# A split-precision encoder layer: the first phase reordered, and the parts of split products taken in another order

## The chip, the cores and the metric

The kernel runs on one core of a Trainium2 chip. The number that counts is the time of one execution on the device, in microseconds (us). A core has several engines that run side by side, each through its own list of instructions in order: TensorE for matrix products (PE in the profile, and PEld for its loads of stationary operands), VectorE (DVE), ScalarE (ACT), GpSimd (POOL) and SyncE (SP), which mostly sends for transfers. Sixteen DMA engines carry the transfers. TensorE writes its results to PSUM, eight banks of 128 partitions by 512 float32 numbers; all other data stand in the larger SBUF or in DRAM.

## The reference

Two sequences (here batch 0 and batch 1) of 1024 rows and 1024 channels go separately through one layer:

```python
xn = rmsnorm(x, g_pre)
p = xn @ w_in                                  # 8192 columns
fv, fg, hv, hg, mg = split(p)                  # 1024, 1024, 3072, 1024, 2048
fz = fft over the sequence and over groups of 256 channels, of fv; real part
y_f = (fz * silu(fg)) @ w_fourier_out
hv = short_conv(hv, w_short); v, x1, x2 = split(hv)
z = v
for n, gate in enumerate((x1, x2)):
    z = gate * long_conv(z, kf[:, n], hyena_d[n])   # over 2L points
y_h = (z * silu(hg)) @ w_hyena_out
g_f, g_h = split(sigmoid(mg + b_merge))
out = (g_f * y_f + g_h * y_h) @ w_out
return x + rmsnorm(out, g_post)
```

The filters kf come from a small network over positions (two hidden layers with a sine each, then exponentials), transformed to frequencies.

## The kernel before

**Split products.** Every large product is made of float32 operands cut in two: a rounded part h, made by ACT (`copy`, a CAST in the profile), and the remainder l = source - h, made by DVE or POOL (a TENSOR_TENSOR at line 181). `split` (L168) does both and keeps the ACT instruction as `self.rounded`. A product is then three passes of TensorE: weight h on data h, weight h on data l, weight l on data h. `mm3` (L372) issues the three, for one block of 128 inner channels after the other, and so before the change the remainder of the weight is needed two products after its rounded part.

**The phases, in order.** `phase_fourier` (L486) makes the Fourier branch of both batches and the hidden layers of the filter network. `phase_main` (L868) makes the filters, with some of the gate projections between them, and then calls `branches` (L908): 32 convolutions (two batches, two orders, eight channel tiles). One convolution is `conv_front` (transposes and butterflies on DVE) and `conv_back` (L796), which calls `forward` (L593, frequency products pX, with DVE's bh and bl as data), multiplies by the filter, splits the result into yh and yl, and goes back with products pT. Its input comes from `inproj` (L727): a PSUM tile pin of 1024 columns, weights wh and wl, data xh and xl, which `load_x` (L714) makes of the normalized, transposed x (d_x in DRAM); the tiles of x are loaded anew for the second batch. `phase_gates` (L996) makes gate projections of batch 1 by a seven-product scheme (`times`, L979, PSUM tile pg). `phase_out` (L1108) makes the two output projections of the branches (`project`, L1147, pyf and pyh) and, in `last_rows`, the last projection and norm.

**The Fourier phase.** It works in five steps for each batch b.

- `norm` (L303) loads the eight row blocks of x (128 rows each), squares each on ACT (Square with a sum, output sq), makes the reciprocal roots of four sums at a time on DVE (`rstd`), and writes eight diagonal matrices dg. For batch 0 the row blocks stay in SBUF; for batch 1 they pass through three buffers of the tag "x".
- `xtile` (L327), once for each of eight channel tiles k, multiplies eight 128-column blocks of x by the diagonals on TensorE (tpx: transposes and scales at once), evicts them on ACT as xg (two buffers, which the outputs sq of `norm` share), writes xg to d_x over SP's queue, folds the sequence into even and odd halves eo on DVE, and splits these into eh and el. Row 512 of the sequence is kept apart in x5, by two very small DVE operations for each k.
- `weights` (L360) loads 128 rows of the Fourier weights (wfv), folds them into wer and wor, and splits these into the resident even and odd weights we and wo. There are two halves of the weights; batch 0 takes half 0 and then half 1, batch 1 takes half 1, which is still there, and then half 0 again.
- `pfv` (L378) adds the 3 products of one channel tile to one of eight sums for each half: e = 0 (even, four row tiles m) and e = 1 (odd, four). For batch 0 and half 0 six sums are begun within the loop over channel tiles: the four even ones in the four "mm" banks and two odd ones in the two "X" banks, while the transposes tpx use the two "T" banks. For batch 1 nothing is begun; there tpx uses the "mm" banks. The sums not begun follow in `fourier_half` (L383).
- `fourier_half` splits the sums as they close, adds a product pfx of x5 with the even weights, evicts that as x5t, and goes through the sequence stages (`stage`, L420: PSUM tiles pse and pso, eviction sev, result sst, products with the large table seq) and the channel stages (pP, pQ, with the table chan; DVE makes fA and fB, which POOL's queue writes to d_fz).

`hidden` (L273) makes one hidden layer of the filter network: two products phd, seven DVE operations each and a Sin on ACT, at the end of which SP's queue writes it to DRAM. Layer 0 stands at the very start, layer 1 after the last half of batch 1. The tables seq, alt, chan and chx are sent for on POOL's queue and vec on SP's, all in the code after the loop of batch 0; a one-column POOL copy into seq and into chan, which reads the last row scales, holds these two back until the norm is done.

**What sets the order of the work.** Not the code's order alone: a planner simulates the program and lists each engine's instructions by when they could start in the simulation, with program order between equals. `tc.issue_after(ins)` keeps instructions from being listed before another one. In the kernel before, the whole second `norm` stands in `issue_after(behind.ins)`, where `behind` is the last rounding of the weights of half 1 (L514, L540). Transfers that one engine sends for go through its queue in the order of its list: SP's queue carries x, wfv, d_x and later nearly all loads; POOL's carries tables, d_fz and weights of the later phases; ACT's queue carries two small loads at the start.

## Time and profile before

| | |
|---|---|
| median of 3 runs | 2446.82 us (2443.44 to 2447.43) |
| the profiled execution | 2449.26 us, of it 2447.1 us span |
| PE busy | 2396.1 us, 98% of the span |
| PEld busy | 2082.3 us, 85% |
| DVE busy | 1893.8 us, 77% |
| ACT busy | 1096.8 us, 45% |
| POOL busy | 485.9 us, 20% |
| Transfers | 429.36 MB, mean 175 GB/s |

The span runs from the first to the last instruction that the profile records; the time of the execution is a little longer. The Fourier phase takes the first 224 us of the span. Busy shares are means over the whole span, and stages differ, so stretches of it have to be read one by one.

A row for a group of instructions reads: source line, engine, operation, output<-input, partitions x elements and type, count, then busy us in all and the mean ns of one, and then the idle time of that engine just before them with what ended it. A row for one instruction begins with its start in us and its duration in us, and ends with the idle time before it and what released it. A row for a stretch has its bounds, its length, the busy us of PE, PEld, DVE, ACT and POOL (with counts), the granted TensorE clock, the busy share of the DMA engines and the GB/s moved. A row of waits has the engine, the waiting tile and line, what released it, and then the total, count and longest in us. A row of the chain has a start, a duration and the work that the end depended on. A row for transfers has the count, the size of one, and the median us from its issue to its landing.

### The profile page before, as it was taken

Reading aid. Unit: us, or ns where it says so; the run is one execution under the profiler, and the core shown is the slowest. Engines: PE = TensorE matmul, PEld = TensorE weight load, DVE = VectorE, ACT = ScalarE, POOL = GpSimd, SP = SyncE. Lnnn points to the kernel's source line nnn. Section 1 sums busy time; section 2 is a strip of 40 time slices with the busy share of each in tenths; the row PEclk is TensorE's granted clock in tenths of the full one; section 3 lists DMA queues with packets and bytes.
Section 4 is the critical chain, followed back from the end, with each engine's and each line's share of the span. In section 5 each row is a group of like instructions: output and inputs, shape, how many; then the busy total and the mean of one; then the engine's idle time right before and its main releaser. Section 6 shows DMA issues by size and latency. Waiting matters only on the chain.

```text
span 2447.1 us, 36853 instructions
## 1 busy us (share of the span) xinstructions
PE 2396.1 (98%) x13196; PEld 2082.3 (85%) x13196; DVE 1893.8 (77%) x3405; ACT 1096.8 (45%) x2063; POOL 485.9 (20%) x516
## 2 busy tenths in 40 slices
PE   6999999999999999999999999999999999999998
PEld 5988888888888888888888888888788888888886
DVE  7687888888748999999989999766555455665677
ACT  5545677767633433334223333333344444544343
POOL 1341222222143433331000000112200111122111
PEclk9999999999999999999999999999999999999999
DMA  7545655555555555445434444335454567776543
GB/s 273 170 141 191 224 175 173 167 175 167 173 194 177 172 177 173 165 165 192 146 128 134 141 141 138 121 121 184 154 174 159 198 210 255 245 250 213 169 164 129
DMA packets 225151, 429.36 MB, mean 175 GB/s; under 512 B 23542, under 2 KB 87255, under 8 KB 224456
## 3 DMA queue, kind: packets, MB, share of 16 engines
q1 hardware_dynamic: 198444, 333.34, 41.1%
q0 software_dynamic: 26336, 93.65, 10.9%
q8 instruction: 104, 1.70, 0.3%
q14 instruction: 79, 0.65, 0.1%
q10 hardware_dynamic: 188, 0.02, 0.0%
HBM read 290.60 MB, written 136.31 MB: 174 GB/s over the span
## 4 chain that ended last, share of the span: by engine, by line
PE 88%; DMA 5%; issue 3%; DVE 2%; ACT 1%; POOL 1%; SPq 0%; DVEq 0%; POOLq 0%; ACTq 0%
PE pin L194 41%; PE pT L194 7%; PE pg L194 7%; PE pX L194 7%; PE po L194 6%; PE pyh L194 5%; PE pyf L194 5%; PE pXf L194 3%; PE pfv L194 2%; DMA wr<-in_w_fo 1%; PE pft L194 1%; PE tph L792 1%; DMA wr<-in_w_ho 1%; PE tpx L194 1%; DMA wfv<-in_w_fv 1%
## 5 line engine op out<-in xcount | busy, mean ns | idle before, releaser
L194 PE MATMUL pin<-xh,wl 128*128 128x512 f32 x1472 | 577.2, 392 | 2.6 <-POOL wl L181 2.6
L194 PE MATMUL pin<-xl,wh 128*128 128x512 f32 x1472 | 575.6, 391 | 2.4 <-DVE xl L181 2.4
L194 PE MATMUL pin<-xh,wh 128*128 128x512 f32 x1472 | 576.5, 392 | 0.7 <-DMA wh<-d_w 0.7
L181 POOL TENSOR_TENSOR wl<-wr,wh 128x512 fp32r<-128x512 f32 x136 | 240.3, 1768 | 1144.0 <-ACT wh L171 1105.9
L194 PEld LDWEIGHTS pin<-xh,wl 128*128 128x128 f32 x1472 | 277.1, 188 | 54.9 <-POOL wl L181 4.1
L194 PEld LDWEIGHTS pin<-xl,wh 128*128 128x128 f32 x1472 | 277.1, 188 | 54.3 <-DVE xl L181 3.2
L194 PEld LDWEIGHTS pin<-xh,wh 128*128 128x128 f32 x1472 | 277.1, 188 | 52.1 <-DMA wh<-d_w 1.1
L171 ACT CAST wh<-wr 128x512 fp32r<-128x512 f32 x264 | 162.8, 619 | 346.0 <-PE pin L194 136.8
L194 PE MATMUL pT<-cinv,yh 128*128 128x256 f32 x1024 | 193.1, 283 | 0.0
L194 PEld LDWEIGHTS pT<-cinv,yh 128*128 128x128 f32 x1024 | 164.0, 190 | 9.0
L181 DVE TENSOR_TENSOR t<-pX,k 128x1024 f32<-128x1024 f32 x128 | 155.9, 1218 | 10.9 <-PE pX L194 9.3
L194 PE MATMUL pX<-bh,cfwd 128*128 128x256 f32 x768 | 159.6, 286 | 0.0
L181 DVE TENSOR_TENSOR wl<-wr,wh 128x512 fp32r<-128x512 f32 x128 | 87.2, 687 | 93.5 <-ACT wh L171 93.2
L194 PE MATMUL pyf<-sf,wh 128*128 128x512 f32 x512 | 158.0, 390 | 0.9 <-ACT wh L171 0.9
L194 PE MATMUL pyh<-sh,wh 128*128 128x512 f32 x512 | 157.3, 389 | 0.0
L171 ACT CAST bh<-b 128x512 fp32r<-128x512 f32 x144 | 89.0, 620 | 126.7 <-DVE b L181 84.5
L194 PE MATMUL pT<-cinv,yl 128*128 128x256 f32 x512 | 144.9, 283 | 0.0
L171 ACT CAST yh<-y 128x512 fp32r<-128x512 f32 x128 | 79.2, 619 | 114.1 <-DVE y L181 91.3
L194 PEld LDWEIGHTS pX<-bh,cfwd 128*128 128x128 f32 x768 | 126.3, 190 | 2.5
L194 PEld LDWEIGHTS pyf<-sf,wh 128*128 128x128 f32 x512 | 96.0, 188 | 21.3 <-ACT wh L171 1.6
L194 PEld LDWEIGHTS pyh<-sh,wh 128*128 128x128 f32 x512 | 96.1, 188 | 19.9
L194 PE MATMUL pX<-bl,cfwd 128*128 128x256 f32 x384 | 109.6, 285 | 0.0
(354 smaller groups left out, 5262.7 us busy)
## 6 DMA issues: line engine op xcount, KB each, us to landing
k<-d_k SPq DMA_DIRECT2D x128, 512.0 KB, 4.0
wr<-in_w_in SPq DMA_DIRECT2D x136, 256.0 KB, 3.1
d_g<-gt SPq DMA_DIRECT2D x124, 256.0 KB, 2.6
d_k<-kt SPq DMA_DIRECT2D x128, 128.0 KB, 2.1
d_k<-kt SPq DMA_DIRECT2D x64, 256.0 KB, 2.3
wr<-in_w_fo POOLq DMA_DIRECT2D x64, 256.0 KB, 4.0
g<-d_g SPq DMA_DIRECT2D x64, 256.0 KB, 4.2
wr<-in_w_ho POOLq DMA_DIRECT2D x64, 256.0 KB, 3.7
```

Of the source, the lines that this page charges most:

```text
L171: self.rounded = nc.scalar.copy(h, src)
L181: return e.tensor_tensor(out, a, b, op=op)
L194: return self.nc.tensor.matmul(out, lhsT, rhs, start=start, stop=stop, skip_group_check=shared)
L792: nc.tensor.transpose(tp[:, q * P:(q + 1) * P], eo[:, e, q], self.ident)
```

## The change

Nine things change, in four groups; the number of matrix products stays.

*In the start of batch 0.* `hidden` returns its Sin and its write to DRAM as a function, which is called after the last Square. The row blocks of x are sent for on SP's and ACT's queues in turn, and the first rows of the weights after the fifth block. `weights` is cut in three (`weight_rows`, `weight_sums`, `weight_parts`): the first sums stand ahead of the last group of diagonals, all first parts and all later weights behind the last diagonal. The groups of diagonals are 4, 3 and 1. `rstd` takes its two small tiles from shared tags.

```diff
-        nc.scalar.activation(out, y, AF.Sin)
+        return lambda: nc.scalar.activation(out, y, AF.Sin)
...
             self.xs.append(x)
+            if b == 0:
+                (nc.scalar if m % 2 else nc.sync).dma_start(x, a[f"x{b}"][m * P:(m + 1) * P, :])
+                if m == 4:
+                    raw = self.weight_rows(pw, 0, 0)
+        lo = 0
+        for m in range(8):
+            x = self.xs[m]
+            if b:
+                nc.sync.dma_start(x, a[f"x{b}"][m * P:(m + 1) * P, :])
             sq = px.tile([P, D], F32, tag="xg", name="sq", bufs=2)
-            nc.scalar.activation(sq, x, AF.Square, accum_out=ss[:, m:m + 1])
-            if m % 4 == 3:
-                q = slice(m - 3, m + 1)
-                self.rstd(px, rs[:, q], ss[:, q], 4)
-                for j in range(m - 3, m + 1):
-                    nc.vector.tensor_scalar(dg[:, j], self.ident, rs[:, j:j + 1], None, op0=MUL)
+            with tc.issue_after(marks[(0, 0, 0, 1, 1, 1, 2, 2)[m]].ins) if b else ExitStack():
+                self.squared = nc.scalar.activation(sq, x, AF.Square, accum_out=ss[:, m:m + 1])
+            if m == 7 and b == 0:
+                raw = self.weight_sums(pw, raw, True)
+            if m in ((3, 6, 7), (3, 7))[b]:
+                q = slice(lo, m + 1)
+                self.rstd(px, rs[:, q], ss[:, q], m + 1 - lo)
+                for j in range(lo, m + 1):
+                    self.scaled = nc.vector.tensor_scalar(dg[:, j], self.ident, rs[:, j:j + 1], None, op0=MUL)
+                lo = m + 1
+        if b == 0:
+            with tc.issue_after(self.scaled.ins):
+                self.weight_parts(W, 0, raw, True)
...
     def weights(self, pw, W, half, k, first):
...
+        self.weight_parts(W, k, self.weight_sums(pw, self.weight_rows(pw, half, k), first), first)
+
+    def weight_rows(self, pw, half, k):
         w = pw.tile([P, 2, 2, 130], F32, tag="wfv", name="wfv", bufs=2)
...
+        return w
+
+    def weight_sums(self, pw, w, first):
...
+        return we, wo
+
+    def weight_parts(self, W, k, sums, first):
+        for i, (r, t) in enumerate(zip(sums, W)):
+            self.split(t[0][:, k], t[1][:, k], r.rearrange("p a b -> p (a b)"), "pool" if i and not first else "dve", "act")
```

*In the loops over channel tiles.* Row 512 is only copied by ACT, into one column of r5 for each tile, and split once after the loop. The tables are sent for at tile 4, held back until that tile's xg. At tile 7 of batch 0 two more odd sums are begun, in the "T" banks, with their first seven tiles of channels; batch 1 begins two even sums at its first tile, in two of the four "mm" banks.

```diff
+        self.xg = xg
...
-        x5 = fo["x5"][:, k]
-        self.split(x5[:, b:b + 33:32], x5[:, 2 + b:35 + b:32], xg[:, 512:513].to_broadcast([P, 2]), "dve", "dve")
+        nc.scalar.copy(fo["r5"][:, k:k + 1], xg[:, 512:513])
...
+                else:
+                    for m in range(2):
+                        begun[0, m] = self.psum("mm", 4, "pfv0")
                 for k in range(8):
-                    if b == 0:
-                        self.weights(pw, W, 0, k, True)
+                    if b == 0 and k:
+                        with tc.issue_after(self.scaled.ins):
+                            self.weights(pw, W, 0, k, True)
                     self.xtile(b, k, px, fo)
...
+                    if (b, k) == (0, 4):
+
                         nc.sync.dma_start(self.vec, a["c_vec"])
                         for t in ("seq", "chan"):
-                            nc.gpsimd.tensor_copy(fo[t][:, 0, 0:1], self.rs[:, 7:8])
+                            nc.gpsimd.tensor_copy(fo[t][:, 0, 0:1], self.xg[:, 0:1])
                         nc.gpsimd.dma_start(fo["seq"], a["c_seq"])
...
+                    if (b, k) == (0, 7):
+
+                        for m in (2, 3):
+                            begun[1, m] = self.psum("T", 2, "pfv1")
+                            for j in range(7):
+                                self.pfv(begun[1, m], 1, m, j, W, fo)
+                    for (e, m), p in begun.items():
+                        self.pfv(p, e, m, k, W, fo)
+                r5 = fo["r5"].unsqueeze(2).to_broadcast([P, 8, 2])
+                self.split(fo["x5"][:, :, b:b + 33:32], fo["x5"][:, :, 2 + b:35 + b:32], r5, "dve", "act")
```

*Between the halves.* The Squares of batch 1 no longer wait for the last rounding of the weights of half 1: blocks 0 to 2 stand behind the rounding of an odd sum of half 0, blocks 3 to 5 behind that of the second weight tile, 6 and 7 behind that of the sixth. The product pfx takes an "mm" bank instead of an "X" bank. The second hidden layer is made ahead of the odd sums of the last half instead of after that half.

```diff
+                if (b, half, e, m) == (1, 1, 1, 0):
+                    self.hidden(1, px, pf)()
...
+                if (e, m) == (1, 1):
+                    self.odd = self.rounded
...
-                        p5 = self.psum("X", 2, "pfx")[0:36, :260]
+                        p5 = self.psum("mm", 4, "pfx")[0:36, :260]
...
-                        behind = self.rounded
+                            if b == 0 and k in (1, 5):
+                                marks.append(self.rounded)
                     self.fourier_half(b, half, W, fo, px, pf, begun)
                     begun = {}
-                    if (b, half) == (1, 1):
-                        self.hidden(1, px, pf)
+                    if b + half == 0:
+                        marks = [self.odd]
```

*The order of the three passes* in `forward`, `inproj`, `conv_back`, `times` and `project`: all passes with the rounded part come first, over the inner tiles of a weight block, and those with the remainder after them. In `inproj` 16 products with wh (two column halves, four inner tiles, xh and xl) stand ahead of the 8 with wl; before, each inner tile had its three together.

```diff
-            for n in range(2):
-                for kk in range(4):
-                    k = 4 * q + kk
+            for w, xs in ((h, (self.xh, self.xl)), (l, (self.xh,))):
+                for n in range(2):
                     s = slice(512 * n, 512 * n + 512)
-                    self.mm3(ps[:, s], (h[:, kk], l[:, kk]), (self.xh[k][:, s], self.xl[k][:, s]), k == 0, k == 7)
+                    for kk in range(4):
+                        k = 4 * q + kk
+                        for x in xs:
+                            self.mm(ps[:, s], w[:, kk], x[k][:, s], w is h and x is self.xh and k == 0, w is l and k == 7)
```

More of the change, by code (lines that the diff above doesn't have):

```diff
@@ L496, in phase_fourier @@
             fo["x5"] = pc.tile([P, 8, 36], F32R, name="x5")
+            fo["r5"] = pc.tile([P, 8], F32, name="r5")
             fo["x5t"] = pc.tile([P, 260], F32R, name="x5t")
@@ L608, in forward @@
         for i, pr in enumerate(pairs):
-            self.mm3(X[:, i], tab(pr, 0), (h[:, 0:2], l[:, 0:2]), True, False)
-            self.mm3(X[:, i], tab(pr, 1), (h[:, 2:4], l[:, 2:4]), False, True)
+            for d, parts in ((h, (0, 1)), (l, (0,))):
+                for k in range(2):
+                    for t in parts:
+                        self.mm(X[:, i], tab(pr, k)[t], d[:, 2 * k:2 * k + 2], d is h and k + t == 0, d is l and k == 1)
         return X
```

67 lines of the change are left out of this document (36 added, 31 removed).

## Prediction

> **What bounds the kernel now.** I read the page first, then busy time in stretches, then TensorE's own waits, the chain of the first 70 us, and single rows where a cause was missing. The page, then stretches of 100 us (bounds and length, then busy time of PE, PEld, DVE, ACT and POOL, granted clock, DMA share, GB/s):
>
> ```profile
> span 2447.1 us, 36853 instructions
> ```
> ```profile
> PE 2396.1 (98%) x13196; PEld 2082.3 (85%) x13196; DVE 1893.8 (77%) x3405; ACT 1096.8 (45%) x2063; POOL 485.9 (20%) x516
> ```
> ```profile
> 0.00:100.00 100.00, 76.26 (x552) 71.94 (x553) 72.12 (x202) 59.08 (x117) 21.77 (x41) 0.97 0.67 224
> 100.00:200.00 100.00, 94.87 (x775) 91.49 (x774) 79.38 (x178) 48.25 (x101) 34.64 (x38) 1.00 0.44 148
> 200.00:300.00 100.00, 94.96 (x548) 82.64 (x547) 75.84 (x158) 61.95 (x123) 20.91 (x21) 1.00 0.63 226
> 800.00:900.00 100.00, 100.00 (x609) 89.24 (x608) 98.57 (x150) 38.14 (x69) 38.15 (x36) 1.00 0.51 172
> 2400.00:2500.00 100.00, 37.38 (x165) 30.60 (x164) 31.85 (x80) 14.94 (x33) 5.83 (x5) 0.96 0.17 60
> ```
>
> TensorE idles 51.0 us in all (2447.1 - 2396.1): 23.7 in the first hundred, 5.1 and 5.0 in the next two, 9.7 in the last 47.1, and 7.5 in the 2,100 between. The change keeps the number of matmuls, so it can only win idle time, and most of that lies in the Fourier phase (0 to 224 us). TensorE's waits name it (us in total, times, longest):
>
> ```profile
> PE tpx L194 <- DMA wfv<-in_w_fv: 9.8, 1, 9.8
> PE tpx L194 <- DVE dg L325: 5.1, 1, 5.1
> PE tpx L194 <- ACT xg L344: 3.5, 2, 2.6
> PE phd L297 <- DMA hd_w<-in_filt_w: 3.5, 1, 3.5
> PE pso L194 <- DVE sst L181: 2.7, 3, 1.3
> PE pin L194 <- POOL wl L181: 2.6, 3, 1.4
> PE pse L194 <- DVE x5t L181: 2.5, 2, 2.1
> PE pin L194 <- DVE xl L181: 2.4, 2, 1.8
> PE pP L194 <- issue: 2.3, 1, 2.3
> PE pQ L194 <- DVE fB L177: 2.0, 1, 2.0
> PE pyh L194 <- DVE wl L181: 1.2, 1, 1.2
> ```
>
> They are waits of single pieces, at a few places; no engine but TensorE is short over the whole span.
>
> **The change part by part.** *First diagonals.* The first products of the loop need all eight diagonals, so of the waits above the 5.1 for dg is the one that decides. The table load and two Sin leave the Squares' way, and the weights' DVE work leaves the second norm chain (now two wer, two wor and a we and wo pair stand in it; at the 0.43 us of the wer below, six take 2.6). Against that, in the new order of issue DVE takes wer and wor, which need the first wfv, ahead of the first norm chain, and ACT their two casts ahead of Squares 5 to 7; and wfv stands in SP's queue behind three row blocks instead of eight, with three more coming beside it on ACT's queue.
>
> ```profile
> 17.86 0.43 DVE L181 TENSOR_TENSOR wer<-wfv 128x260 f32<-128x260 f32 x1 [0.25 <-DMA wfv<-in_w_fv]
> ```
> ```profile
> 0.00:31.30 31.30, 12.73 (x53) 9.56 (x53) 21.25 (x71) 18.90 (x33) 4.15 (x15) 1.00 0.82 292
> 31.30:62.00 30.70, 28.07 (x224) 27.87 (x224) 25.15 (x54) 17.78 (x29) 3.71 (x8) 0.94 0.75 252
> ```
>
> Bounds: -2.6 (the chain cleared) and +3 (wfv no earlier than now, and both chains behind it). At 292 GB/s and a DMA share of 0.82 the 4.2 MB of x cannot come much faster, so I take 0. [...] No run here shows two loaded hardware queues.
>
> *Loop over channel tiles, batch 0.* The chain of waits, an issue, and the issues of d_x up to 36 us and from 38 to 58:
>
> ```profile
> 28.77 8.87 DMA d_x<-xg
> ...
> 38.49 4.57 PE tpx L194 x24
> ...
> 49.35 1.78 PE tpx L194 x16
> ...
> 55.77 6.43 PE pfv L194 x54
> ```
> ```profile
> 24.41 0.53 POOL L532 DMA_DIRECT2D seq<-in_c_seq  x1 [0.18 <-POOL chan L531]
> ```
> ```profile
> d_x<-xg SPq DMA_DIRECT2D x2, 512.0 KB, 8.9
> ```
> ```profile
> d_x<-xg SPq DMA_DIRECT2D x6, 512.0 KB, 3.1
> ```
>
> A product takes 6.43/54 = 0.119 us, a transpose record 1.78/16 = 0.111. From 31.3, when the loop's products begin, to 62.0, when they end, TensorE had 8 x 18 products (17.1) and the transposes of five tiles, 5 x 16 records (8.9): 26.0 us of work in 30.7 (second row above), so 4.7 were lost. The cause is the large seq table, sent for at 24.41: beside it the first two writes of d_x took 8.9 us instead of the 3.1 of the later six, and the third xg, with 38.49's transposes behind it, waited for its buffer. The change sends for seq only after tile 4, when all but the last weights have been asked for. What is late next: the d_x writes of tiles 5 to 7. They are covered by the 42 products of the two further odd sums (5.0 us), which now stand ahead of tile 7's; without that cover the 4.7 come back. I take -4.5, bounds -4.7 and 0. Of the 4.7, 24 x (0.190 - 0.111) = 1.9 are the slow transposes at 38.49, just after an idle stretch of 2.6. [...]
>
> *Stages of batch 0, second half, and the rest of the phase.*
>
> ```profile
> 90.35 1.06 ACT L320 ACTIVATE sq<-x 128x1024 f32<-128x1024 f32 x1 [3.39 <-DMA x<-in_x]
> ```
> ```profile
> 82.00:100.00 18.00, 15.46 (x113) 14.97 (x113) 13.06 (x47) 13.59 (x31) 3.79 (x7) 0.91 0.76 246
> 112.00:150.00 38.00, 33.80 (x281) 32.45 (x281) 34.27 (x64) 23.95 (x41) 17.00 (x16) 1.00 0.63 216
> 150.00:170.00 20.00, 20.00 (x170) 19.88 (x170) 10.84 (x31) 6.15 (x18) 2.29 (x5) 1.00 0.19 75
> 170.00:190.00 20.00, 19.07 (x144) 17.17 (x143) 19.42 (x39) 7.98 (x20) 11.67 (x14) 1.00 0.27 86
> 206.00:224.00 18.00, 13.25 (x97) 11.43 (x95) 12.21 (x25) 11.93 (x21) 1.05 (x2) 1.00 0.93 323
> ```
> ```profile
> L173 DVE CAST x<-xg 128x2 fp32r<-128x2 f32 x8 | 5.2, 658 | 0.0
> L181 DVE TENSOR_TENSOR x<-xg,x 128x2 fp32r<-128x2 f32 x8 | 2.5, 321 | 0.1
> ```
>
> 82 to 100 (idle 2.5): pP's wait has no named cause; in it ACT waits 3.39 for a late row block of batch 1, with sev and px queued behind. The Squares of batch 1 now start after an odd sum's rounding and lie between the weight casts, so that one goes; but weight casts and the first sev then queue behind Squares whose row blocks (three buffers) may still be on the way. -1, bounds -2.5 and +3.4.
>
> 112 to 150 (idle 4.2, DVE 34.27 of 38): the loop of batch 1, bound by DVE. It loses 16 tiny DVE operations (5.2 + 2.5 = 7.7 us, now eight one-column ACT copies and one split behind the loop), and TensorE gets 2 x 24 = 48 products early, 5.7 us, out of a stretch (150 to 170) where it never idles. The two sums hold two of the four "mm" banks that the transposes use. -4, bounds -4.2 and +2.3 (as long as pP waited above, for banks). 170 to 190 (idle 0.9): the second hidden layer moves out of DVE's fullest stretch, 19.42 of 20, to an earlier one: -0.5, bounds -0.9 and +0.9.
>
> 206 to 224 (idle 4.75): x5t's product pfx no longer shares its banks with pP and pQ and is issued among the odd sums, so its 2.1 goes, and with it a gate: the reload of x's tile 1 waits for pfx to release the even weights. pQ's 2.0 came from fB, at a place where reloads and writes run at 323 GB/s. New: four stages follow each other without filler. -3.5, bounds -4.75 and +1.5 (the longest wait of pso for sst was 1.3).
>
> *Order of products in the main, gate and output phases.* Rounded parts first, remainders last. In the input projection the remainder wl is now needed 16 products after wh, not 2. The step of a 512-column product, from the chain:
>
> ```profile
> 1742.17 165.71 PE pg L194 x731
> ```
>
> 165.71/731 = 0.227 us, so wl has 3.6 us where it had 0.45; the longest such wait was 1.4. Those waits go: 2.6 + 1.2 = -3.8, bounds -3.8 and 0. The other side: the first pass over a fresh x takes a tile every 2 products instead of 3, so at the two reloads (xl, 2.4 now) it meets the data earlier, by 3 x 0.227 = 0.7 each: +1, bounds 0 and +2. Elsewhere TensorE does not idle, and order gains nothing.
>
> Sum: 0 - 4.5 - 1 - 4 - 0.5 - 3.5 - 3.8 + 1 = -16.3. The profiled execution took 2449.26 us (span 2447.1 and 2.2 around it), 2.4 above the median 2446.82; from the median: 2430.5.
>
> **The rivals.** *The late stretches give nothing*: 112 to 150 and 206 to 224 stay bound by DVE and by 323 GB/s of reloads, and 82 to 100 only moves. Then -4.5 - 3.8 + 1 = -7.3: 2439.5. For it: the DVE and DMA shares; against: 7.7 us leave DVE.
>
> *Queues held up at the start*: DVE stands before wfv and ACT before row blocks: +3 for 0, +3.4 for -1, so -8.9: 2438. For it: both run in order and wfv landed at 17.8; against: wfv is now asked for earlier.
>
> *Slower: DVE becomes the bound of the convolutions.* From 800 to 900 it is busy 98.57 of 100 beside a TensorE that never idles, and its order inside a convolution changes there. If each of the 32 convolutions lost 0.8 us, that is +25.6 against -16.3: 2456. It decides from 16.3/32 = 0.51 us each. Against it: bl and yl are needed three and two products later than now, so TensorE forgives more.
>
> *More than forecast*: every part at its better bound, -2.6 - 4.7 - 2.5 - 4.2 - 0.9 - 4.75 - 3.8 = -23.5: 2423.4. For it: most of the idle time named above is addressed; against: each part has a successor ready.
>
> *The change not doing what it says* is excluded by the order of issue, where the begun sums, the moved Squares and the late remainders stand as written.
>
> **How the numbers follow.** Chances: forecast 0.36, late stretches 0.19, held-up queues 0.12, more 0.09, slower 0.24. The likeliest gives 2430.5, with 2425 to 2436 as its own range (the doubtful bounds of one part). The range begins at 2423 and takes in the milder third of the slower case, up to 0.66 us for each convolution (32 x 0.66 - 16.3 = 4.8: 2452), which leaves out 0.16. A difference of 0.2% (4.9 us, 2441.9 and 2451.7) is about what a measurement of this kernel tells from none. Faster: 0.36 + 0.09, two thirds of the late and of the held-up case together (their times lie 2 to 4 us inside that bound), 0.66; same: the other third, 0.10; slower: its case, 0.24.
>
> **What would show it.** Right: the third xg within 4 us of its write; the loop of batch 0 ended near 58 and the odd sums with it by 63; no ACT wait of 3 us on a row block in batch 1; no wait on x5t, none on wl above 0.2; the first pin some 12 us earlier. Wrong: the second group of diagonals after 25; ACT waiting for x ahead of a sev; TensorE under 99.5 of 100 anywhere from 300 to 1,100 us, where the slower rival would stand.

## The result, and the profile after

The changed kernel is slower: median 2453.51 us of 12 runs (2448.92 to 2458.21) against 2444.61 us of 12 runs of the kernel before (2442.61 to 2450.08), ratio 1.0034 with a 95% interval of 1.0026 to 1.0042. That is 8.9 us more; 16.3 less were forecast. The profiled execution took 2453.49 us. The one of the kernel before, on which the sum was made, was a long one: 2449.26 us, 4.7 above the median of the 12.

The page of the changed kernel, then its busy time by stretches (columns as in the prediction: PE, PEld, DVE, ACT, POOL, clock, DMA share, GB/s):

```profile
span 2451.7 us, 36907 instructions
...
PE 2399.9 (98%) x13196; PEld 2080.8 (85%) x13196; DVE 1912.3 (78%) x3384; ACT 1099.6 (45%) x2081; POOL 504.0 (21%) x516
```
```profile
0.00:62.00 62.00, 44.47 (x314) 40.48 (x315) 46.76 (x120) 37.82 (x73) 14.76 (x23) 1.00 0.77 271
62.00:112.00 50.00, 45.66 (x368) 43.35 (x367) 35.61 (x110) 27.91 (x69) 14.41 (x20) 1.00 0.48 150
112.00:150.00 38.00, 31.21 (x256) 29.86 (x255) 35.25 (x50) 24.80 (x49) 18.53 (x18) 1.00 0.71 244
150.00:300.00 150.00, 147.38 (x963) 132.76 (x962) 114.25 (x249) 82.17 (x178) 43.54 (x40) 1.00 0.52 180
```
```profile
800.00:900.00 100.00, 100.00 (x607) 89.03 (x606) 99.86 (x147) 38.49 (x70) 37.22 (x37) 1.00 0.53 167
900.00:1000.00 100.00, 97.89 (x591) 86.33 (x591) 99.77 (x149) 36.20 (x64) 32.04 (x32) 1.00 0.55 173
1000.00:1100.00 100.00, 97.11 (x573) 84.37 (x572) 99.86 (x145) 35.84 (x67) 37.55 (x32) 1.00 0.47 148
```

The same stretches of the kernel before, for the Fourier phase:

```profile
0.00:62.00 62.00, 40.81 (x276) 37.43 (x276) 46.40 (x124) 36.68 (x62) 7.86 (x23) 0.97 0.79 272
62.00:112.00 50.00, 47.46 (x379) 46.52 (x378) 32.98 (x102) 26.53 (x66) 15.04 (x20) 0.97 0.47 149
112.00:150.00 38.00, 33.80 (x281) 32.45 (x281) 34.27 (x64) 23.95 (x41) 17.00 (x16) 1.00 0.63 216
150.00:300.00 150.00, 144.03 (x940) 129.68 (x940) 113.68 (x250) 82.12 (x175) 37.42 (x41) 1.00 0.51 182
```

TensorE has about the same products to do in both kernels, so its busy time in a stretch that begins at 0 tells how far it has come (busy time at a lower clock counts in full: in the kernel before a transpose record took 0.190 us from 38.49 us on, at a clock of 0.63, and 0.111 from 49.35 on, at 1.00; so the two rows at 0.97 flatter that kernel a little). The first 62 us gained 3.7 us of work. The next two stretches gave 1.8 and 2.6 back, and the last gained 3.4. Over 300 us that is 2.6 ahead of this execution of the kernel before. The experiments e1, e3 and e4 below keep the old Fourier phase, and so show it again; they have 267.7, 268.6 and 269.6 us of work in 300, where the kernel before shows 266.1 and the changed kernel 268.7. Against the mean of those four, 268.0, the changed Fourier phase gained 0.7 us. The four differ by up to 3.5 among themselves, so that is nearly nothing.

From 800 to 1,100 us VectorE is now busy without a break, and TensorE, which did not idle there before, idles 5.0 us. The waits of TensorE (total, times, longest):

```profile
PE tpx L194 <- DVE dg L342: 12.2, 2, 11.3
PE pfv L194 <- ACT eh L171: 4.2, 5, 1.2
PE pyf L194 <- ACT wh L171: 4.0, 3, 2.2
...
PE pfx L194 <- DVE x L181: 3.0, 1, 3.0
PE pfv L194 <- DVE we L181: 2.6, 3, 1.4
PE pT L194 <- DVE yl L181: 2.1, 3, 1.6
```

The first products now wait 11.3 us for a diagonal, where they waited 9.8 for wfv and then 5.1 for dg. The other waits that the prediction named (x5t, fB, wl) are gone from the list. Others stand in their place: eh, we and the late split of row 512 in the Fourier phase, yl in the convolutions, wh in the output phase.

### The profile page after: what moved, and what is told of

Its sections match the earlier page's. It is cut to its first block, busy times and chain, and to the rows that moved or that the text cites. A ratio compares the mean times of both kernels' runs of the same rounds, so it can differ in the third digit from the quotient of the medians.

```text
span 2451.7 us, 36907 instructions
## 1 busy us (share of the span) xinstructions
PE 2399.9 (98%) x13196; PEld 2080.8 (85%) x13196; DVE 1912.3 (78%) x3384; ACT 1099.6 (45%) x2081; POOL 504.0 (21%) x516
## 4 chain that ended last, share of the span: by engine, by line
PE 52%; DVE 6%; DMA 2%; issue 1%; ACT 1%; SPq 0%; DVEq 0%; ACTq 0%
PE pin L194 17%; PE pg L194 8%; PE po L194 6%; PE pyf L194 6%; PE pyh L194 5%; PE pT L194 5%; PE pX L194 4%; DMA g<-d_g 1%; DVE b L181 1%; DVE x L177 1%; DVE t L181 1%; PE tph L847 1%; DMA oraw<-in_w_out 1%; DVE yl L181 0%; DVE bl L181 0%
## 5 line engine op out<-in xcount | busy, mean ns | idle before, releaser
L181 POOL TENSOR_TENSOR wl<-wr,wh 128x512 fp32r<-128x512 f32 x136 | 247.8, 1822 | 945.4 <-PE pin L194 753.9
L194 PE MATMUL pin<-xh,wl 128*128 128x512 f32 x1472 | 383.0, 391 | 0.0
L194 PE MATMUL pT<-cinv,yh 128*128 128x256 f32 x1024 | 165.2, 284 | 2.8 <-ACT yh L171 1.6
L194 PEld LDWEIGHTS pT<-cinv,yh 128*128 128x128 f32 x1024 | 145.1, 190 | 11.3 <-ACT yh L171 4.0
L194 PE MATMUL pyf<-sf,wh 128*128 128x512 f32 x512 | 127.7, 392 | 4.0 <-ACT wh L171 4.0
L194 PE MATMUL pX<-bh,cfwd 128*128 128x256 f32 x768 | 131.0, 287 | 0.0
L194 PE MATMUL pyh<-sh,wh 128*128 128x512 f32 x512 | 126.9, 390 | 0.2
L194 PEld LDWEIGHTS pX<-bh,cfwd 128*128 128x128 f32 x768 | 110.3, 190 | 3.9
L181 DVE TENSOR_TENSOR bl<-b,bh 128x512 fp32r<-128x512 f32 x144 | 104.0, 724 | 6.4 <-ACT bh L171 6.2
L194 PE MATMUL pT<-cinv,yl 128*128 128x256 f32 x512 | 104.1, 285 | 2.2 <-DVE yl L181 2.1
```

What stands on the lines that cost most here:

```text
L181: return e.tensor_tensor(out, a, b, op=op)
L194: return self.nc.tensor.matmul(out, lhsT, rhs, start=start, stop=stop, skip_group_check=shared)
```

## The experiments

All times are medians; the ratio is that to the kernel before, measured on the same chip in the same session. The ratio is taken over all runs and not from the two medians, so the two can differ somewhat: e1 is 8.4 us slower by the medians and 0.29%, or 7.1 us, by the ratio. Runs of different sessions are best compared by their ratios. A profile shows one execution; that of e2 took 3.4 us more than the median of its runs, that of e6 4.3 us less.

| run | what it is | us | ratio, 95% interval |
|---|---|---|---|
| after | the changed kernel | 2453.51 | 1.0034 (1.0026 to 1.0042) |
| e1_order_only | before + new order of products | 2452.88 | 1.0029 (1.0017 to 1.0041) |
| e2_fourier_only | after, old order of products | 2453.23 | 1.0037 (1.0024 to 1.0051) |
| e3_order_inproj | before + new order in the input projection | 2447.45 | 1.0018 (1.0009 to 1.0027) |
| e4_order_conv | before + new order in forward and conv_back | 2444.39 | 1.0001 (0.9992 to 1.0010) |
| e5_start_only | before + the changed start and loop of batch 0 | 2448.48 | 1.0017 (1.0008 to 1.0025) |
| e6_squares_back | after, second norm put back | 2446.28 | 1.0009 (1.0000 to 1.0017) |
| e7_no_b1_sums | after without the two even sums | 2454.30 | 1.0039 (1.0025 to 1.0052) |
| e8_x5_back | after, row 512 split for each tile | 2455.64 | 1.0040 (1.0027 to 1.0054) |
| e9_before_wl_act | before, wl a second rounded copy by ACT (the remainder is left out) | 2439.67 | 0.9980 (0.9971 to 0.9989) |
| e10_after_wl_act | after, the same replacement | 2446.08 | 1.0003 (0.9993 to 1.0012) |
| e11_sq_back_old_order | e6 + old order of products | 2447.98 | 1.0013 (1.0004 to 1.0022) |
| e12_sq_back_conv_order | e11 + new order in forward, conv_back, times | 2448.62 | 1.0018 (1.0009 to 1.0026) |
| e13_sq_back_inproj | e11 + new order in the input projection | 2441.06 | 0.9984 (0.9975 to 0.9994) |
| e14_project_back | after, old order in the output projections | 2447.88 | 1.0015 (1.0007 to 1.0024) |

### Is it the order of products or the Fourier phase?

The first four runs take the two halves of the change apart, and then the order by places. For e1 the five functions of the changed kernel replace those of the kernel before; e2 is the reverse:

```diff
 # e1: forward, inproj, conv_back, times, project as in the changed kernel; e2: these five as before
-    self.mm3(ps[:, s], (h[:, kk], l[:, kk]), (self.xh[k][:, s], self.xl[k][:, s]), k == 0, k == 7)
+    for w, xs in ((h, (self.xh, self.xl)), (l, (self.xh,))):
...
```

> The kernel before with the new order of products alone (all five functions), the Fourier phase as before. Theory A, the order costs the convolutions of batch 0: from the two traces +7.4 us between 700 and 1,130 us (VectorE over 99 of 100 busy, its SBUF-only operations stretched beside GpSimd), -3 at 1,700 to 1,740, +4.2 in the output phase, so 8 to 12 us slower than before. Theory B, the convolutions lose because the Fourier phase hands over at another time and the order of products is harmless: within 3 us of before.

> The changed kernel with the old order of products, so the Fourier phase alone is changed. Theory A: the 4 to 6 us that the trace of the changed kernel shows gained by the first input projection stay, 4 to 6 us faster than before, and VectorE stays under 98 of 100 between 800 and 1,100 us. Theory B: the loss in the convolutions comes with the shifted start, 4 to 9 us slower than before.

> The kernel before with the new order in the input projection alone. If the loss comes from GpSimd's remainders wl starting at another point of a convolution (the last product with wl now ends the block): 4 to 8 us slower than before, VectorE over 99 of 100 between 800 and 1,100 us. If it comes from the order inside the convolution: about 3 us faster than before, by the waits for wl at 1,712 and 1,730 us.

> The kernel before with the new order in the frequency products and the way back alone. If the loss comes from the order inside the convolution (VectorE's list changed, since bl and yl are needed later): 4 to 8 us slower than before. If it comes from the input projection: within 2 us of before.

Measured: each half alone is about as slow as both together (e1 8.4 us, e2 8.8 above the kernel before in their session). Neither theory foresaw that: e1 is as slow as theory A said, e2 as slow as theory B said. e3 is 3.0 us slower by the medians and 4.4 by the ratio, the lower end of its first case, with VectorE at 98.4 of 100 instead of over 99; e4 came out as its second case. In the stretch from 800 to 1,100 us theory A held. The rows of the kernels in the order before, after, e1, e3, e4:

```profile
800.00:1100.00 300.00, 300.00 (x1824) 267.96 (x1822) 291.07 (x451) 113.67 (x205) 110.18 (x106) 1.00 0.51 169
```
```profile
800.00:1100.00 300.00, 295.00 (x1768) 259.74 (x1767) 299.50 (x439) 110.53 (x200) 106.81 (x101) 1.00 0.51 163
```
```profile
800.00:1100.00 300.00, 296.67 (x1787) 262.84 (x1785) 298.66 (x447) 113.90 (x206) 113.96 (x103) 1.00 0.50 167
```
```profile
800.00:1100.00 300.00, 299.38 (x1820) 266.63 (x1819) 295.31 (x450) 116.79 (x208) 115.66 (x104) 1.00 0.51 169
```
```profile
800.00:1100.00 300.00, 300.00 (x1822) 267.73 (x1821) 292.63 (x453) 115.23 (x209) 106.19 (x104) 1.00 0.51 170
```

VectorE fills the 300 us where the order is new everywhere (299.5 and 298.7), and TensorE idles for it; with the old order (e2, 300.0 us of TensorE and 293.7 of VectorE, too), or with the new one in the convolutions alone, TensorE does not idle. The input projection's order alone stands between (295.3, idle 0.6). So the order makes the convolutions of batch 0 much dearer only where it is new in the projection and in the convolution. From the first of the 256 transposes tph to the 129th, the first of batch 1, the kernels take 471.2 us (before), 479.0 (after), 475.4 (e1), 470.7 (e2), 472.6 (e3) and 470.3 (e4). The runs below repeat this: four more with the new order in both places take 475.9 to 477.6 (e6, e7, e8, e14), three with the old order in the projection 470.3 to 470.8 (e5, e11, e12), and e13, like e3, 472.2. The changed kernel's 479.0 is the longest of the six with the new order; their mean is 476.7. Batch 1, whose weights wl come ready from DRAM, loses nothing: from the 129th transpose to 1,684 us the two kernels stay 4 us apart.

e2 is slow elsewhere: its first tph starts at 705.6 us, that of the changed kernel at 694.5. Up to 700 us TensorE idles 6.0 us more in e2, 5.0 of them between 224 and 300 us: with the old order, the first input projections after the new end of the Fourier phase wait for wl (3.1 us in one wait) and, for less, for xl and xh. Besides, the granted clock in e2's profile was 0.77 from 140 to 155 us and 0.89 from 270 to 285, where the changed kernel has 1.00; by these shares that is up to 5.1 us more (an estimate, 15 x 0.23 + 15 x 0.11). The wait for wl returns in e11, and its cause is shown there.

### What makes VectorE slower

The number of VectorE's operations in a convolution is the same in both kernels. Groups of VectorE by shape between 700 and 1,170 us, the kernel before and then the changed one (busy us and mean ns):

```profile
L181 DVE TENSOR_TENSOR t<-pX,k 128x1024 f32<-128x1024 f32 x62 | 75.4, 1216 | 4.6 <-PE pX L194 3.8
...
L181 DVE TENSOR_TENSOR bl<-b,bh 128x512 fp32r<-128x512 f32 x48 | 32.9, 702 | 0.0
...
L181 DVE TENSOR_TENSOR b<-xt,bs 128x256 f32<-128x256 f32 x32 | 12.9, 440 | 0.0
```
```profile
L181 DVE TENSOR_TENSOR t<-pX,k 128x1024 f32<-128x1024 f32 x61 | 74.0, 1213 | 0.2
...
L181 DVE TENSOR_TENSOR bl<-b,bh 128x512 fp32r<-128x512 f32 x46 | 36.0, 785 | 0.0
...
L181 DVE TENSOR_TENSOR b<-xt,bs 128x256 f32<-128x256 f32 x32 | 21.9, 720 | 0.0
```

The product t, one source of which lies in PSUM, takes the same time in both. Several of the operations with both sources in SBUF are longer, the two shown most; a few are shorter (`b<-bs,xt` 450 ns instead of 551). A place in the changed kernel shows it, first VectorE and then GpSimd (start and duration of each row):

```profile
888.71 0.67 DVE L181 TENSOR_TENSOR T0s<-T0s,pT 128x512 f32<-128x512 f32 x1
889.31 1.19 DVE L181 TENSOR_TENSOR yl<-y,yh 128x512 fp32r<-128x512 f32 x1
890.42 2.94 DVE L181 TENSOR_TENSOR b<-xt,bs 128x256 f32<-128x256 f32 x2
```
```profile
888.25 3.40 POOL L181 TENSOR_TENSOR x<-x,sg 128x512 f32<-128x512 f32 x2 [2.64 <-ACT sg L1009]
891.61 1.48 POOL L181 TENSOR_TENSOR wl<-wr,wh 128x512 fp32r<-128x512 f32 x1
```

While GpSimd multiplies and subtracts, the PSUM operation keeps its 0.67 us, but yl takes 1.19 (0.68 at 883.23 us, with no GpSimd arithmetic beside it) and two operations on 256 elements take 2.94, which without GpSimd beside them take 0.41 each. From 700 to 1,170 us of this kernel the 22 operations `b<-xt,bs` with no GpSimd arithmetic beside them take 0.41 to 0.42 us; the 10 that have it beside them for more than half of their time take 1.40 in the mean and up to 1.91. For bl these means are 0.68 (32 operations) and 1.17 (10). The product t takes 1.21 to 1.23 with it and without.

So the same GpSimd work costs more or less, by what VectorE happens to do beside it. Call the stretch of VectorE's operations the time by which they exceed the 20th percentile of their own shape, summed (not to be taken for the stretches of time in the rows above). Over batch 0's convolutions it is 28.8 us before, 28.4 in e2, 30.0 in e4, 34.8 in e3, 38.8 in e1 and 43.9 in the changed kernel, with 107 to 114 us of GpSimd's arithmetic in all of them. What moved GpSimd's work can be read from what ended its waits before wl, between 700 and 1,170 us, in the kernel before and then in the changed one:

```profile
L181 POOL TENSOR_TENSOR wl<-wr,wh 128x512 fp32r<-128x512 f32 x47 | 83.6, 1779 | 245.8 <-ACT wh L171 242.5 <-PE pin L194 3.3
```
```profile
L181 POOL TENSOR_TENSOR wl<-wr,wh 128x512 fp32r<-128x512 f32 x46 | 80.6, 1753 | 70.9 <-PE pin L194 59.7 <-issue 11.1
```

Before, the subtraction starts as soon as ACT has rounded wh. In the changed kernel the products with wl end a block of the projection, and the subtraction starts when a product pin releases the buffer that it is to fill. e4 is like the kernel before in this (239.3 us of its waits end with wh), e1 and e3 like the changed one (66.6 and 42.4 us end with pin). That is what the expectation of e3 named. Why the convolution's own order has to be new too for the full loss is not shown.

The next pair takes GpSimd's wl away:

```diff
-                self.split(*parts, r, "pool", "act")
+                self.nc.scalar.copy(parts[0], r)
+                self.nc.scalar.copy(parts[1], r)
```

> The kernel before, with GpSimd's subtraction for wl in the input projection replaced by a second rounded copy on ScalarE; the remainder of the weights is left out, so the result differs, and the products are as many. GpSimd then computes nothing beside the convolutions but the product with the gate. Theory (VectorE's operations with both sources in SBUF are stretched while GpSimd computes): the stretch of VectorE's operations between the first transposes of batch 0 and of batch 1, 28.8 us now, falls to under 12, and that stretch stays at 468 to 471 us, since TensorE was the bound. Rival (the order of VectorE's list decides, not GpSimd): the same as before with the stretch as it is.

> The changed kernel with the same replacement. Theory: the stretch of VectorE's operations, 43.9 us, falls to under 14, the convolutions of batch 0 go from 479.0 to 469 to 472 us, and the kernel is 5 to 8 us faster than the changed one. Rival: they stay at 476 us or more with TensorE idle for 4 us or more, since the new order of the products holds VectorE up without GpSimd too.

The rows of e9 and e10:

```profile
800.00:1100.00 300.00, 300.00 (x1821) 268.08 (x1820) 276.33 (x448) 132.30 (x236) 54.74 (x73) 1.00 0.50 168
```
```profile
800.00:1100.00 300.00, 300.00 (x1823) 267.98 (x1823) 281.64 (x453) 133.69 (x240) 51.29 (x72) 1.00 0.50 170
```

The stretch falls to 9.7 us in e9 and 9.4 in e10, and batch 0's convolutions take 468.6 and 467.0 us, so without GpSimd's subtraction the new order is no longer dearer there (1.6 us cheaper). That settles the convolutions. The two kernels still differ by 0.23% (before and after: 0.34%), which lies in the other places.

### What becomes of the gain of the first loop

e5 keeps only the new start and loop of batch 0; e6 puts the second norm back behind the last weight rounding; e7 and e8 undo one part each.

```diff
 # e6, in the changed kernel
-                self.norm(b, px, pf, pw, W, marks if b else None)
+                with tc.issue_after(behind.ins) if b else ExitStack():
+                    self.norm(b, px, pf, pw, W, [behind] * 3)
...
 # e7
-                else:
-                    for m in range(2):
-                        begun[0, m] = self.psum("mm", 4, "pfv0")
 # e8 (the split after the loop goes)
-        nc.scalar.copy(fo["r5"][:, k:k + 1], xg[:, 512:513])
+        x5 = fo["x5"][:, k]
+        self.split(x5[:, b:b + 33:32], x5[:, 2 + b:35 + b:32], xg[:, 512:513].to_broadcast([P, 2]), "dve", "dve")
...
```

> The kernel before with only what the change does up to the end of the loop of batch 0 (Sin deferred, two queues, first weights, groups of 4, 3 and 1, table seq at tile 4, the two further odd sums of half 0); Squares, pfx, row 512, hidden layer, batch 1 and the order of products as before. In the traces the 192nd product pfv starts at 63 us in the changed kernel and at 68 to 70 in the kernels with the old start. If that gain is kept and only the later steps lose: 4 to 6 us faster than before. If the next stage has to wait for the weights of half 1 whatever the Squares do, because it only comes earlier: within 2 us of before.

> The changed kernel with the second norm behind the last weight rounding again, as before. In the changed kernel TensorE waits for half 1's weights between 71 and 84 us (3.6 us of gaps), while row blocks of batch 1 stand between the weight rows on SP's queue and their chain between the weights' sums on VectorE. If the moved Squares cause that: 3 to 5 us faster than the changed kernel. If the gain of the loop is given back anyway: within 1.5 us of the changed kernel.

> The changed kernel without the two even sums begun in the loop of batch 1. If they give nothing, since that loop is set by VectorE and the early products only wait for eh (4.2 us of waits in five places): within 1.5 us of the changed kernel. If they win what the prediction gave that stretch: 3 to 5 us slower than the changed kernel.

> The changed kernel with row 512 split for each channel tile on VectorE again, instead of copied and split after the loop. The wait of pfx for that split (3.0 us) goes, and 7.7 us of small VectorE operations come back into the loops. If the late split costs: 2 to 3 us faster than the changed kernel. If VectorE's time in the loop counts: 2 to 4 us slower.

e6 is the largest single step back: 7.2 us under the changed kernel, 0.25% by the ratios, somewhat more than expected. Its first 300 us hold 272.9 us of work against 268.7:

```profile
0.00:62.00 62.00, 44.73 (x313) 41.05 (x314) 46.57 (x120) 37.70 (x72) 14.76 (x23) 1.00 0.77 272
62.00:112.00 50.00, 47.39 (x392) 46.04 (x391) 38.08 (x116) 29.62 (x72) 16.72 (x21) 1.00 0.52 160
112.00:150.00 38.00, 33.04 (x275) 31.97 (x275) 31.50 (x52) 24.85 (x49) 17.00 (x20) 1.00 0.66 230
```

It keeps the gain of the first loop, and loses less in the two stretches after it. The other profiles agree: the first product pin starts at 209.2 to 212.3 us in the four kernels with the second norm put back (e6, e11, e12, e13), and at 215.6 to 219.9 in the six with the moved Squares (after, e2, e7, e8, e10, e14). SP's queue in the changed kernel, from 64 us:

```profile
64.13 3.56 SPq L332 DMA_DIRECT2D x<-in_x  x3
69.64 0.33 SPq L387 DMA_DIRECT2D wfv<-in_w_fv  x1
...
75.15 3.20 SPq L387 DMA_DIRECT2D wfv<-in_w_fv  x2
```

Row blocks of batch 1 go out ahead of and between the last four weight rows of half 1, which are sent for at 69.6, 70.6, 75.1 and 78.0 us; in e6 these go at 68.4, 69.3, 72.1 and 73.6, and no row block between them. VectorE forms the last sum wer of half 1 at 82.4 us in the changed kernel and at 76.3 in e6. So the weights of half 1 are 6 us late, and TensorE, which needs them from 71 us on, waits piece by piece. Row blocks on SP's queue, Squares on ACT and the norm's chain on VectorE move together with the Squares, and the traces show the first two at work on the fifth of the eight weight rows. It is sent for 1.2 us later than in e6, since it waits for a buffer, and so for a VectorE operation that waits for a cast behind a Square on ACT; and it takes 4.5 us to land instead of 2.7, beside the row blocks. The other 3 us build up over the last three rows. Which of the three costs TensorE most was not told apart.

e7 shows that the two even sums in the loop of batch 1 give nothing (0.8 us slower without them, within the intervals). VectorE sets the pace of that loop, and it is no faster there: it loses the small operations of row 512, but the folding eo, beside GpSimd's half of it, takes 1.60 us each instead of 0.80 (kernel before, then changed, 105 to 150 us):

```profile
L181 DVE TENSOR_TENSOR eo<-xg 128x512 f32<-128x512 f32 x8 | 6.4, 797 | 2.5 <-ACT xg L344 2.5
```
```profile
L181 DVE TENSOR_TENSOR eo<-xg 128x512 f32<-128x512 f32 x8 | 12.7, 1604 | 1.5 <-ACT xg L365 1.5
```

e8 is 2.1 us slower than the changed kernel; the intervals overlap, so that row 512 gains in the whole is likely and not shown. Its part in the loop of batch 0 is clearer. The 192nd product pfv, the last of half 0, starts at 68.2 us in e8 and at 70.1 in e5, which both split row 512 for each tile, and at 62.2 to 63.9 in the nine other kernels with the new start (68.2 to 69.6 in the five with the old one). e5 fell outside both expectations: 4.0 us slower than before. Its trace has a wait of 4.5 us of pfv for an xg in the loop of batch 0, which the changed kernel has not. In the changed kernel the write d_x of tile 5 is sent for at 42.5 us and the table seq at 46.1; in e5 the table goes at 44.6 and that write 2.2 us after it, beside the table. How such a write fares the changed kernel shows: those sent for behind the table, at 48.4 and 53.1 us, took 10.6 and 10.3 us to land, the one at 38.5, ahead of it, 2.6. In e8, which differs from the changed kernel in row 512 alone, the same wait is 2.8 us. The rows of e5:

```profile
PE pfv L194 <- ACT xg L365: 4.5, 1, 4.5
```
```profile
44.64 0.54 POOL L569 DMA_DIRECT2D seq<-in_c_seq  x1
```
```profile
46.86 3.43 SPq L367 DMA_DIRECT2D d_x<-xg  x2
```

So the new place of the table, behind tile 4, is a race with a margin of 3.6 us, and what keeps it is the small VectorE work taken out of the loop. In part it does so by a delay that nobody planned: GpSimd's one-column copy into seq, which holds the table back, takes 8.49 us in the changed kernel,

```profile
37.34 8.49 POOL L570 CAST seq<-xg 128x1 fp32r<-128x1 f32 x1 [1.92 <-ACT xg L365]
```

while VectorE works without a break beside it; the like copy into chan behind it takes 0.18. In e5 and e8, where the small operations of row 512 stand between VectorE's others, the copy into seq takes 2.56 and 2.53. At 0.18 us the table would have gone out some 8 us earlier, ahead of that write (an estimate from these rows).

### What remains of the order, and the output phase

> The changed Fourier phase with the second norm behind the last weight rounding, and the old order of products everywhere. If the loss is the sum of the moved Squares (6 to 7 us) and of the order in the convolutions (6 to 8) and in the output phase (about 3): 5 to 8 us faster than before, 2437 to 2440. If the first input projections wait for wl behind the new end of the Fourier phase, as they did in the kernel with the Fourier phase alone changed (9 us more between 220 and 400 us): no faster than before.

> The same, with the new order kept in the frequency products, the way back and the gate phase, and the old order in the input and output projections. By the run with the order inside the convolution alone, which moved nothing: within 2 us of the kernel with the old order everywhere.

> The changed kernel with the second norm behind the last weight rounding, and the new order of products kept in the input projection alone. The sum of what the runs showed: the Fourier phase of the kernel with the norm moved back (6 us less lost than in the changed kernel by 300 us), no wait for wl behind it (that came with the old order in the input projection), batch 0's convolutions at 472 to 473 us instead of 476 to 479, and the output phase without the new order of its weights. 3 to 5 us faster than before, 2439.5 to 2442. If the output phase or the convolutions lose as much with the input projection's order alone: 2445 or more.

> The changed kernel with the old order of products in the two output projections alone. Between 2,050 and 2,300 us the kernels with the new order there lost 3 to 10 us to waits of pyf for wh, those with the old order 1 to 4. If the order does that: 3 to 5 us faster than the changed kernel. If these waits are late transfers that come whatever the order: within 1.5 us of it.

The edits are the functions named in the table, taken from the one or the other kernel. e11 came out as its second case, 3.3 us slower than before. TensorE's wait and the GpSimd instruction it waits for:

```profile
PE pin L194 <- POOL wl L181: 3.1, 1, 3.1
```
```profile
258.11 8.42 POOL L181 TENSOR_TENSOR wl<-wr,wh 128x512 fp32r<-128x512 f32 x1 [3.39 <-ACT wh L171]
```

The stretching has another side: this subtraction, 1.28 to 1.34 us in seven of its nine places between 220 and 285 us of that trace, takes 8.42 here, among VectorE's filter work. With the old order wl is needed 2 products after wh, and TensorE stands; with the new one it has 16, and e13, which has it, does not wait for wl there. e12 gains nothing over e11, as expected.

e13 joins what gained: the new Fourier phase with the second norm put back, and the new order in the input projection alone. It takes 2441.06 us, 4.6 under the kernel before (2445.63 in that session) and 12.4 under the changed one, as the sum of the causes had it. It is the fastest kernel of the study that computes the whole. Batch 0's convolutions take 472.2 us in it.

e14 is 5.6 us under the changed kernel (0.19%, or 4.6 us, by the ratios, whose intervals do not overlap). So the new order in the output projections costs, as expected. From 2,050 to 2,300 us, the changed kernel and e14:

```profile
2050.00:2300.00 250.00, 245.72 (x1068) 200.74 (x1067) 143.98 (x222) 111.09 (x186) 48.04 (x88) 0.99 0.70 231
```
```profile
2050.00:2300.00 250.00, 247.94 (x1090) 203.95 (x1090) 148.84 (x228) 114.74 (x192) 47.93 (x89) 1.00 0.70 232
```

The waits are those of pyf for wh (4.0 us against 0.9). In both kernels ACT has a Sigmoid for a late gate ahead of the rounding of wh. Why the new order waits longer for it was not tried. The other profiles agree with the loss: in this window TensorE idles 2.7 to 6.7 us in the six kernels with the new order in the output projections, 0.2 to 2.3 us in the ten with the old one.

## Why the prediction was wrong

*Sign and size.* 2453.51 lies just above the range, which ended at 2452, and on the other side of the forecast. The rival that ended slower, VectorE as the bound of the convolutions, at 0.24, was the mechanism of one of the three causes. Of the other two, the moved Squares had a price for ACT alone, and the output projections had none. One sign of being wrong that the prediction named came true: TensorE was busy 97.9 and 97.1 of 100 us between 900 and 1,100. The first product pin came 3.6 us earlier, not 12.

*The order of products: "elsewhere TensorE does not idle, and order gains nothing".* This step failed. The order was counted by what TensorE waits for, not by where it puts GpSimd's work against VectorE's, at a place where VectorE had 3 of 100 us left. Against the rival's 0.8 us for each of 32 convolutions, measured were (479.0 - 471.2)/16 = 0.49 each, in the 16 of batch 0 alone, and less in the five other kernels with the new order. The argument against it, that bl and yl are needed later, did not bear: the loss is VectorE's own time. The trace of before held the price: between 700 and 1,300 us x<-yc,invn,x takes 2.31 to 2.39 us in six places, all beside a GpSimd operation, and 1.27 or 1.28 in the twelve others, ten of them without one.

*"-3.8" for the waits for wl.* Right where it was meant: the waits at 1,712 and 1,730 us are gone, and 1,700 to 1,760 us show 60.0 us of work instead of 57.5. With the new order in the input projection alone (e3, e13) the gate products pg wait there for a wl of their own instead, 2.7 and 1.8 us. "+1" for the reloads of x was too much: the waits for xl are 1.6 us now, 2.4 before.

*The output projections* stood in the sum at nothing beyond wl; measured is a loss of 4.6 to 5.6 (e14).

*"0" for the first diagonals, "-4.5" for the loop of batch 0.* Right, the second in part by luck. The 192nd pfv, the last product of the half, starts at 63.1 us instead of 69.6 (68.2 to 69.6 in the three repeats). The cover named for the late d_x writes, the odd sums, held, but only with the table sent for behind the write of tile 5: by a margin that e5 and e8 show to be small, and that owes much to the copy of 8.49 us, which the prediction did not have. With x sent for on two queues the first 31.3 us moved 268 GB/s (292 before), so a second queue brought no bandwidth here.

*"-1" for 82 to 100 us.* Wrong in sign. The stretch from 62 to 112 us lost 1.8 us of work against the kernel before (2.8 against the mean of the four). The bound +3.4 was for weight casts held up behind Squares on ACT. What the traces show is the weights of half 1 late as a whole, by 6 us, with row blocks between their rows on SP's queue and the norm's chain between their sums on VectorE; the moved Squares had a price on ACT, and these two had none. Also, the wait of 2.3 us without a cause that was to go there is in the execution shown and in none of the three repeats.

*"-4" for the loop of batch 1.* Wrong in sign: 2.6 us of work less in the stretch (2.2 against the mean). The 7.7 us of row 512 left VectorE, half of them here, but 6.3 us came back as stretch of eo; the late split, costed at nothing, makes pfx wait 3.0; the 48 early products gave nothing (e7).

*"-0.5" and "-3.5" for the end of the phase.* Right in sign, nearly in size: 150 to 300 us has 3.4 us more work (2.6 against the mean of the four), and no wait for x5t or fB is left.

*The 1.9 us of slow transposes behind the pause of 2.6 us.* The prediction counted them as a gain. The pause is gone, and the granted clock from 36 to 46 us is 1.00 instead of 0.83. But e3 and e4, with the old start, have 1.00 there too, so these 1.9 us are lost in some executions only.

## What to carry to other kernels

Before an engine's instructions are put in another order near a stretch that VectorE nearly fills (95.7 to 98.6 of 100 us here), count what GpSimd does beside it and which of VectorE's operations read twice from SBUF (here `b<-xt,bs`, which does, went from 440 to 720 ns, and t, with one source in PSUM, from 1216 to 1213). The duration of one shape, with its spread, showed it here before any change: x<-yc,invn,x took 1.27 to 2.39 us. A step that is moved takes its transfers with it, and its followers along, so its price is read on every queue that it enters as well as on its own engine. And a stall found in one profile is worth winning only if it stands in a second one: here 2 to 4 us of the idle time that was to be won belonged to that one execution.

## What the runs showed that was not expected

GpSimd and VectorE stretched each other here by far more than the overlap of two instructions: on GpSimd 1.3 us became 8.42 (e11), and 0.18 became 8.49 (changed kernel); on VectorE 0.41 became 1.5 (changed kernel). Parts of the change are not additive: the order alone costs 8.4 us, the Fourier part alone 8.8, both 8.9, since the new order in the input projection removes a wait that the new Fourier phase creates. That order alone costs 3.0 us on the kernel before (e3) and gains 6.9 on e11 (e13), by the medians.

The granted clock was lower after some pauses of TensorE under 3 us and not after others. After a pause of 2.62 us (kernel before) and of 2.38 (e1) it was 0.83 from 36 to 46 us, after pauses of 2.14 and 2.00 (e4, e3) it was 1.00; but after one of 2.04 at 204.5 us in e4 it was 0.79 from 204 to 212. What makes the difference between them is not shown.
